# Pooling tiles between the modulations' pieces, another mix of split and whole pieces, four splits on another engine, and sums at other places in the heads

## The chip, the cores and the metric

One core of one Trainium2 chip. The metric is the device time of one execution in microseconds (us), and it is the lower the better. Engines are named as in the profile: PE (TensorE, matmuls; PEld are its weight loads), DVE (VectorE), ACT (ScalarE), POOL (GpSimd), SP (the engine whose queue issues most transfers).

## The reference, cut to what matters

The model is one step of a two-layer backbone over 640 tokens of width 1024: 512 latent tokens (a grid of 8 by 64) and 128 context tokens. Layer 0 mixes tokens by pooling, layer 1 by retention with 4 heads; an MLP with a squared ReLU (4096 wide) follows each. Every sub-layer is normed, then scaled and shifted, and its result is gated:

```
mod = silu(cond) @ w_ada[i] + b_ada[i]          # cond: c (latent) or c_ctx (context)
sh_a, sc_a, g_a, sh_m, sc_m, g_m = split(mod, 6)
h = rmsnorm(x, norm_mix_w[i]) * (1 + sc_a) + sh_a
mix = pool_mixer(h) if i == 0 else retention_mixer(h)
x = x + g_a * mix
h = rmsnorm(x, norm_mlp_w[i]) * (1 + sc_m) + sh_m
x = x + g_m * square(relu(h @ mlp_w1[i])) @ mlp_w2[i]
```

So each layer needs six modulations, each a product of two vectors (two kinds of token) with a 1024 x 1024 matrix of `w_ada`: 4 MB of weights per modulation, 48 MB in all, for almost no arithmetic. The pooling mixer takes, per group of 256 channels, the mean over a window of 2, 4, 8 or 16, less the token itself, through a 256 x 256 matrix.

## The kernel before, in words

Activations lie transposed, as eight tiles d = 0..7 of 128 channels by 640 tokens, in two halves of 320 tokens. Products with float32 precision are made of three matmuls of a reduced float32 type (`mm3`, L205 to L207): each operand is split into a high part (`S.copy` on ACT, L144) and the low remainder (a subtraction on DVE, or on POOL where a call says so, L145).

**Modulations.** `ada` (L272) computes them in steps, as a generator. A modulation has two halves of 512 columns and each half four pieces of 256 rows; a step handles one piece. The five modulations of layer 0 that are needed first come in the order 1, 0, 2, 4, 3: 40 pieces, with one load of 1 MB for each two pieces on SP's queue, into five buffers. A letter of `MODES` (L50) says how a piece is multiplied: `p` whole, in plain float32, without other engines; `v` split by ACT and DVE into two parts that PE multiplies with a split vector. All are the matmuls of L283. A piece is multiplied one step late (`LAG`). When a half's four pieces are done, ACT copies the row (L287) and PE turns it (L293, `turn`), one step later again.

**The opening's order** is written out in `PLAN` (L52): `a2` is two steps of the modulations, `l` and `v` load tables, `w3` is pooling tile 3 (`pooled`, L608), and `PLAN[1]` to `PLAN[8]` stand between the eight products of the pooling mixer (`pool_add`, L675). The function `run` (L646) reads a word with `map(int, word[1:])`, which goes through the digits of the word one by one:

```
def run(plan):
    for word in plan.split():
        {"w": pooled, "a": astep, "v": vectors, "l": load_tables}[word[0]](*map(int, word[1:]))
```

So `a10` calls `astep(1, 0)`, and the second argument of a `step` (L402) is `until`: it goes on until modulation 0 is in a set of pairs, which never is, and thus through all pieces to the end of the generator. Pooling tile 0 stands behind all 40 pieces, and the later words `a2` and `a1` find nothing to do.

A pooling tile takes five transposes on PE (L621, L622), eight matmuls with a window matrix (L630) and one for the context (L632), two activations on ACT (L637), four operations on DVE (L638, L639) and a split (L144, L145). Each two tiles share `group` (L593): a load of `iv` on ACT's queue (L596), the window matrix `pm` on DVE (L601), and the split of four 128 x 256 inputs into tiles of the tag `t` (L603 to L605), of which there are seven. The tile also needs modulations 1 and 0 (`a0` and `mod[0][0]`). Matmuls, transposes and sums write PSUM banks of one tag, of which there are eight. A framework orders each engine's instructions by its own estimates; buffers of one tag are given out in program order.

**Then** come the products `pool_add` with `add_to_x` (L500), the sums of squares (`Squares`, L421), the reciprocal root (`rsqrt`, L147 to L159, on DVE), and `norm_tile` (L475), whose tiles (`h0h`, `h0l`, ...) feed the MLP (`mlp`, L749).

**Weights of the MLP** are split by `weights` (L186); `OTHER[i]` (L59) says how many of the first blocks of 128 columns of layer i's MLP have their subtraction on POOL: none in layer 0, four in layer 1.

**The heads.** In layer 1 four modulations are made by `ada_sums` (L375): a step loads 1 MB, multiplies and adds it up on DVE (16 operations of 128 x 256, L387 and L389) in two accumulators that exist once, and the next step first turns the result on PE (four transposes, L394) and reduces it on DVE (L395). There are 16 such sums, so 17 steps. They stand in the loop over heads (L1149 on): a step behind the preparation of attention, one behind the product `gate(0)`, one behind `gate(1)`, one behind `gated`, and in head 0 one more before the output projection, which needs modulation 2 of layer 1. Between heads, `values` (L981) and `queries_keys` make the next head's inputs.

Of the kernel before, what the change touches and what calls it, by code (L numbers as in the profile page):

```python
# [9 lines left out]
F32 = mybir.dt.float32  # L10
# [36 lines left out]

MODES = ("pppp ppvv", "vvpv vpvv", "vvpv vpvp", "vpvp ppvp", "vppv vpvp")  # L50
MODE5 = "s s"
PLAN = ("a2 l a4 v a10 w0 a2 w1 a2 w2 a2 w3 a2 w4 a2 w5 a2 w6 a2 w7",  # L52
        "a1", "a1", "a1", "a1", "a1", "a1", "a1", "a1")
LAG = 1
FIRST = "x x x x x"
LATE = (False, True)
TURN = 5
BACK = 5
OTHER = (0, 4)  # L59
AHEAD = 1  # L60
FREE = 5

# [48 lines left out]
def hybrid_kernel(ctx: ExitStack, tc: tile.TileContext, x_prompt, x_sample, state_ret, c, c_ctx, w_ada, b_ada,  # L111
# [6 lines left out]
    def nm(s):  # L118
        uid[0] += 1
        return f"{s}_{uid[0]}"  # L120
# [254 lines left out]
    def ada_sums(works, place):  # L375


        for i, m in works:
            for q in range(4):
                col = m * D + q * 256  # L380
                w = load(w_ada[i, :, col:col + 256], (8, 256))
                acc = place()
                for k in range(KD):
                    for j in range(2):
                        by = c4[:, k, j:j + 1]
                        if k == 0:
                            V.tensor_scalar(acc[j], w[:, k], by, None, ALU.mult)  # L387
                        else:
                            V.scalar_tensor_tensor(acc[j], w[:, k], by, acc[j], ALU.mult, ALU.add)  # L389
                yield  # L390
                pt = bank()
                for j in range(2):
                    for k in range(2):
                        T.transpose(pt[:, (2 * j + k) * 128:(2 * j + k + 1) * 128], acc[j][:, k * 128:(k + 1) * 128], ident)  # L394
                V.tensor_reduce(mod[i][m][:, q * 2:q * 2 + 2, :], pt.rearrange("p (j n k) -> p n j k", j=2, n=2),  # L395
                                axis=AX.X, op=ALU.add)
            ob = O_B + i * 48 + m * KD
            V.tensor_tensor(mod[i][m], mod[i][m], vec[:, ob:ob + KD].unsqueeze(2).to_broadcast([128, KD, 2]), ALU.add)
            ready.add((i, m))

    def stepper(gen):
        def step(n=1, until=None):  # L402
            while n if until is None else until not in ready:
                try:
                    next(gen)
                except StopIteration:
                    return
                n -= 1
        return step
# [62 lines left out]
    def h_tiles(d, dt=F32R):  # L472
        return [hp.tile([128, TOK], dt, tag=f"h{d}{e}", name=nm(f"h{d}{e}")) for e in "hl"]
# [56 lines left out]
    def follow(sq, norm, items):  # L530


        r = []

        def products(item, h, mid=None):
            return gemm([w() for w in item[0]], item[1], h, mid)

        out = products(items[0], 0, lambda: r.append(sq.rstd()))
        splits = []
        for d in range(KD):  # L540
            splits.append(norm(1, d, r[0]))
            if d:
                splits[d - 1]()
        splits[-1]()
        items[0][2](0, out)
        for h in range(2):
            for item in items[1 - h:]:
                item[2](h, products(item, h))


    with tc.tile_pool(name="pool", bufs=1) as pp:
# [56 lines left out]
        def pooled(d):  # L608

            if not a0:  # L610
                astep(until=(0, 0))
                a0.append(scale_of(0, 1, O_MIX))
            g = d // 2
            if d % 2 == 0:
                grp[g] = group(g)
            iv, pm, xh, xl = grp[g]
            cols = slice(d * 128, (d + 1) * 128)
            sub = slice(d % 2 * 128, d % 2 * 128 + 128)
            ps, pq, pr = bank(), bank(), bank()
            for i in range(4):  # L620
                T.transpose(ps[:, i * 128:(i + 1) * 128], xt[i][:, cols], ident)  # L621
            T.transpose(pq[:, 0:128], xt[4][:, cols], ident)  # L622
            for i in range(4):

                w = WINDOWS[g]
                lo, hi = max(0, 2 * i - w // 2 + 1), min(ROWS, 2 * i + w // 2 + 2)
                lo, hi = (0, ROWS) if i == 0 else (min(lo, ROWS - 4), max(hi, min(lo, ROWS - 4) + 4))
                o = SPAN // 2 - 1 - 2 * i
                for e, z in enumerate((xh, xl)):
                    T.matmul(pr[:, lo * GRID_W:hi * GRID_W], z[i // 2][:, i % 2, sub], pm[:, o + lo:o + hi, :],  # L630
                             start=(i == 0 and e == 0), stop=(i == 3 and e == 1))
            T.matmul(pq[:, 128:256], xt[4][:, cols], win_sb[:, g * SEQ:(g + 1) * SEQ], start=True, stop=True)  # L632
            n_ = h_tiles(d, F32)[0]
            t = pp.tile([128, TOK], F32, tag="df", name=nm("df"), bufs=2)
            for j, cols, z, mean in ((0, slice(0, LAT), ps, pr), (1, slice(LAT, TOK), pq[:, 0:128], pq[:, 128:256])):
                sc_, sh_ = a0[0][:, d, j:j + 1], mod[0][0][:, d, j:j + 1]
                S.activation(n_[:, cols], z, AF.Identity, scale=sc_, bias=sh_)  # L637
                V.scalar_tensor_tensor(t[:, cols], mean, sc_, iv[:, cols], ALU.mult, ALU.mult)  # L638
                V.scalar_tensor_tensor(t[:, cols], t[:, cols], sh_, n_[:, cols], ALU.add, ALU.subtract)  # L639
            diff.append(split(t, *h_tiles(d)))  # L640
# [4 lines left out]

        def run(plan):  # L646
            for word in plan.split():
                {"w": pooled, "a": astep, "v": vectors, "l": load_tables}[word[0]](*map(int, word[1:]))

        run(PLAN[0])  # L650
        astep(until=(0, 2))
# [258 lines left out]
    with tc.tile_pool(name="ret", bufs=1) as rp:  # L910
# [70 lines left out]
        def values(hd):  # L981

            out = [bank() for _ in range(5)]
            c0 = 2048 + hd * DV
            for e in range(2):
                st = load(ret_w_in[0, e * 512:(e + 1) * 512, c0:c0 + 512], (4, 512))
                for f in range(2):
                    w = split_w(st[:, 2 * f:2 * f + 2])
                    for i in range(5):
                        for k in range(2):  # L990
                            hh = [z[:, i * 128:i * 128 + 128] for z in h1t[e * 4 + f * 2 + k]]
                            first, last = e == 0 and f == 0 and k == 0, e == 1 and f == 1 and k == 1
                            T.matmul(out[i], hh[0], w[0][:, k, :], start=first, stop=False)  # L993
                            T.matmul(out[i], hh[1], w[0][:, k, :], start=False, stop=False)  # L994
                            T.matmul(out[i], hh[0], w[1][:, k, :], start=False, stop=last)  # L995
            vs = [centre(out[i], *[rp.tile([128, DV], F32R, tag=f"v{i}{e}", name=nm("v")) for e in "hl"])
                  for i in range(4)]
            vpr = t5()
            vpc = rp.tile([128, DV], F32, tag="vpc", name=nm("vpc"))
            S.copy(vpr, out[4])  # L1000
            V.tensor_scalar(vpc, vpr, mean_of(vpr), None, ALU.add)
            return vs, split(vpr, t5().bitcast(F32R), t5().bitcast(F32R)), vpc
# [133 lines left out]

        qk, pairs, _ = queries_keys(0)
        follow(sq, norm1, pairs)
        vv = values(0)
        h2 = []  # L1140

        def norm2(h, d, r):
# [1 line left out]
                h2.extend([scale_of(1, 4, O_MLP + KD), mod[1][3], [h_tiles(d) for d in range(KD)]])  # L1144
            return norm_tile(h, d, r, *h2)

        step1 = stepper(ada_sums([(1, 2), (1, 4), (1, 3), (1, 5)], lambda: [rp.tile(
            [128, 256], F32, tag=f"acc{j}", name=nm("acc")) for j in range(2)]))
        for hd in range(HEADS):  # L1149
            gate = gates(hd)  # L1150
            final = states(hd, qk[1], vv[1])
            next(final)
            attn = attention(hd, *qk, vv[0], vv[2])
            step1()
            sg = [gate(0, between=final)]
            step1()
            sg.append(gate(1, between=final))
            step1()
            us = gated(hd, gate, sg, *attn())
            step1()  # L1160
            get = weights(ret_w_out[0, hd * DV:(hd + 1) * DV])
            if hd < HEADS - 1:
                vv = values(hd + 1)
                if hd == 0:
                    step1(until=(1, 2))
                for n in range(KD):
                    for h in range(2):
                        add_to_x(n, h, gemm([get(n)], us, h)[0], mod[1][2])
                qk, _, singles = queries_keys(hd + 1)
                for u in singles:  # L1170
                    u()
            else:
                sq = tail(lambda n, h: gemm([get(n)], us, h)[0], mod[1][2], normed(norm2))
# [74 lines left out]
```

## Time and profile before

| what | value |
|---|---|
| runs shown | 1634.32, 1642.6, 1639.77 us; median 1639.77 us |
| profiled execution, its own time | 1639.26 us |
| its span in the profile | 1637.4 us (mean granted clock of PE 0.991) |
| PE busy | 1585.1 us, 97% of the span |
| DVE busy | 1181.8 us, 72% |
| ACT busy | 703.3 us, 43% |
| POOL busy | 22.6 us, 1% |
| read from memory | 161.43 MB, 103 GB/s over the span |

The profile shows one execution. Busy times say how long an engine had an instruction; a wait is the idle time in front of an instruction, with what ended it. The granted clock is 1.00 at PE's full clock (2.4 GHz) and 0.50 at its half clock (1.2 GHz); a value between is a mean over a stretch.

### The profile page before, as it was taken

The page shows a single profiled execution, that of the slowest core. Times are in us where ns is not written, and L with a number is a line of the kernel's source. Part 1 is how long each engine was busy: PE and PEld are TensorE (multiplying, and loading weights), DVE is VectorE, ACT ScalarE, POOL GpSimd, SP SyncE. Part 2 cuts the span into 40 slices and gives each one's busy share as a digit, 9 for nine tenths or more (in the row PEclk, how much of TensorE's full clock was granted, in tenths as well). Part 3 has the DMA queues.
Part 4 walks back from the last instruction along what each step waited for, and adds up shares of the span by engine and source line. Part 5 has one row for each costly group of instructions (what it writes and reads, how often), then busy time and mean ns, then how long its engine had stood idle before and what let it go on. Part 6 is the DMA issues. An engine that isn't in the chain of part 4 may idle for free.

```text
span 1637.4 us, 24591 instructions
## 1 busy us (share of the span) xinstructions
PE 1585.1 (97%) x9897; PEld 1478.8 (90%) x9897; DVE 1181.8 (72%) x2295; ACT 703.3 (43%) x1287; POOL 22.6 (1%) x30
## 2 busy tenths in 40 slices
PE   7988999999999999999999999999999999999998
PEld 2278999999999998889889988998899999999998
DVE  4499997677667687886986688678966574564654
ACT  5665525416237364333442433243464262351540
POOL 0000000000000000000000000000200000000000
PEclk9999999999999999999999999999999999999999
DMA  9813431333333213324313142223122032131311
GB/s 352 296 57 129 155 104 52 109 124 103 109 98 104 78 43 126 115 78 129 129 52 129 63 145 102 78 91 116 52 77 78 27 109 98 52 104 52 109 59 65
DMA packets 137954, 169.83 MB, mean 104 GB/s; under 512 B 3512, under 2 KB 111472, under 8 KB 137840
## 3 DMA queue, kind: packets, MB, share of 16 engines
q1 hardware_dynamic: 134800, 161.28, 30.0%
q0 software_dynamic: 1312, 4.20, 0.8%
q10 hardware_dynamic: 1728, 2.78, 0.5%
q8 instruction: 78, 1.28, 0.3%
q14 instruction: 36, 0.29, 0.1%
HBM read 161.43 MB, written 6.82 MB: 103 GB/s over the span
## 4 chain that ended last, share of the span: by engine, by line
PE 83%; DVE 8%; DMA 5%; ACT 3%; issue 1%; ACTq 0%; DVEq 0%; SPq 0%
PE ps L205 24%; PE ps L206 24%; PE ps L207 24%; DMA wst<-in_mlp_w_dram 2%; PE ps L995 2%; PE ps L993 2%; PE ps L994 2%; PE ps L283 2%; DVE wlo L145 2%; ACT whi L144 1%; DMA wst<-in_w_ada_dram 1%; DVE acc L389 1%; PE ps L394 1%; DVE xall L500 1%; PE ps L630 1%
## 5 line engine op out<-in xcount | busy, mean ns | idle before, releaser
L144 ACT CAST whi<-wst 128x1024 fp32r<-128x1024 f32 x242 | 251.2, 1047 | 467.0 <-PE ps L206 263.2
L145 DVE TENSOR_TENSOR wlo<-wst,whi 128x1024 fp32r<-128x1024 f32 x238 | 288.1, 1221 | 118.7 <-ACT whi L144 118.0
L206 PE MATMUL ps<-a,whi 128*128 128x320 f32 x896 | 276.9, 310 | 0.8 <-DVE a L145 0.8
L205 PE MATMUL ps<-a,whi 128*128 128x320 f32 x896 | 277.1, 310 | 0.2 <-ACT a L144 0.2
L207 PE MATMUL ps<-a,wlo 128*128 128x320 f32 x896 | 276.2, 309 | 0.0
L500 DVE SCALAR_TENSOR_TENSOR xall<-ps,mod,xall 128x320 f32<-128x320 f32 (+2 forms) x288 | 116.0, 434 | 160.3 <-PE ps L207 159.5
L206 PEld LDWEIGHTS ps<-a,whi 128*128 128x128 f32 x896 | 168.0, 188 | 2.0 <-DVE a L145 1.8
L205 PEld LDWEIGHTS ps<-a,whi 128*128 128x128 f32 x896 | 168.0, 188 | 0.4 <-ACT a L144 0.4
L207 PEld LDWEIGHTS ps<-a,wlo 128*128 128x128 f32 x896 | 168.0, 188 | 0.0
L389 DVE SCALAR_TENSOR_TENSOR acc<-wst,c,acc 128x256 f32<-128x256 f32 x336 | 136.1, 477 | 0.0
L207 PE MATMUL ps<-tq,wlo 128*128 128x320 f32 x288 | 89.0, 309 | 0.0
L205 PE MATMUL ps<-tq,whi 128*128 128x320 f32 x288 | 89.0, 309 | 0.0
L206 PE MATMUL ps<-tq,whi 128*128 128x320 f32 x288 | 89.0, 309 | 0.0
L145 DVE TENSOR_TENSOR a<-t,a 128x320 fp32r<-128x320 f32 x128 | 61.8, 487 | 23.8 <-ACT a L144 23.0
L206 PE MATMUL ps<-A,whi 128*128 128x320 f32 x256 | 79.0, 309 | 0.0
L205 PE MATMUL ps<-A,whi 128*128 128x320 f32 x256 | 78.8, 311 | 0.0
L207 PE MATMUL ps<-A,wlo 128*128 128x320 f32 x256 | 78.5, 309 | 0.0
L855 ACT ACTIVATE t<-t 128x320 f32<-128x320 f32 x128 | 60.5, 473 | 1.3
L144 ACT CAST a<-t 128x320 fp32r<-128x320 f32 x128 | 58.5, 457 | 1.3
L435 ACT ACTIVATE t<-xall 128x320 f32<-128x320 f32 x56 | 26.1, 470 | 70.8 <-DVE xall L500 69.8
L207 PEld LDWEIGHTS ps<-tq,wlo 128*128 128x128 f32 x288 | 54.1, 188 | 0.0
L205 PEld LDWEIGHTS ps<-tq,whi 128*128 128x128 f32 x288 | 54.1, 188 | 0.0
(423 smaller groups left out, 4036.7 us busy)
## 6 DMA issues: line engine op xcount, KB each, us to landing
wst<-in_mlp_w_dram SPq DMA_DIRECT2D x64, 1024.0 KB, 5.3
wst<-in_w_ada_dram SPq DMA_DIRECT2D x46, 1024.0 KB, 5.3
wst<-in_ret_w_in_dram SPq DMA_DIRECT2D x24, 1024.0 KB, 5.2
wst<-in_ret_w_out_dram SPq DMA_DIRECT2D x8, 1024.0 KB, 5.1
t<-in_state_ret_dram SPq DMA_DIRECT2D x16, 256.0 KB, 4.0
out_dram<-t POOLq DMA_DIRECT2D x16, 256.0 KB, 2.6
xt<-in_x_sample_dram SPq DMA_DIRECT2D x4, 512.0 KB, 4.5
both<-in_w_ada_dram SPq DMA_DIRECT2D x2, 1024.0 KB, 7.3
```

What stands on the lines that cost most here:

```text
L144: S.copy(hi, src)
L145: sub.tensor_tensor(lo, src, hi.bitcast(F32), ALU.subtract)
L205: T.matmul(out, wh, ah, start=first, stop=False, skip_group_check=more)
L206: T.matmul(out, wh, al, start=False, stop=False, skip_group_check=more)
L207: T.matmul(out, wl, ah, start=False, stop=last, skip_group_check=more)
L283: T.matmul(pa, lhs[:, kk + k, :], z[:, k, :], start=first and k == 0 and j == 0, stop=last and k == 1 and j == len(w) - 1)
L389: V.scalar_tensor_tensor(acc[j], w[:, k], by, acc[j], ALU.mult, ALU.add)
L500: V.scalar_tensor_tensor(x, ps[:, cols], gate[:, d, j:j + 1], x, ALU.mult, ALU.add)
L855: S.activation(f, r, AF.Square)
L993: T.matmul(out[i], hh[0], w[0][:, k, :], start=first, stop=False)
L994: T.matmul(out[i], hh[1], w[0][:, k, :], start=False, stop=False)
L995: T.matmul(out[i], hh[0], w[1][:, k, :], start=False, stop=last)
```

## The change

Six edits. (1) `run` reads a word's digits as one number. (2) `a10` becomes `a5 a5`, and the plan's other words stay. (3) `MODES` gets other letters: 17 whole pieces where there were 20, one of them among the first 16 (8 before) and 16 among the last 24 (12 before). (4) `n_` in a pooling tile takes one buffer where `h_tiles` took a pair and used one. (5) `OTHER` becomes (0, 0): the four subtractions of layer 1's MLP go from POOL to DVE. (6) In the heads, a first step of the sums comes before `values(0)`; the step behind `gate(0)` stays in head 0 alone; and a step stands behind each `values(hd + 1)` where head 0 alone had one.

```diff
-MODES = ("pppp ppvv", "vvpv vpvv", "vvpv vpvp", "vpvp ppvp", "vppv vpvp")
+MODES = ("pvvv vvvv", "vvvv vvvv", "vpvp vpvp", "ppvp ppvp", "ppvp ppvp")
 MODE5 = "s s"
-PLAN = ("a2 l a4 v a10 w0 a2 w1 a2 w2 a2 w3 a2 w4 a2 w5 a2 w6 a2 w7",
+PLAN = ("a2 l a4 v a5 a5 w0 a2 w1 a2 w2 a2 w3 a2 w4 a2 w5 a2 w6 a2 w7",
         "a1", "a1", "a1", "a1", "a1", "a1", "a1", "a1")
...
-OTHER = (0, 4)
+OTHER = (0, 0)
...
-            n_ = h_tiles(d, F32)[0]
+            n_ = hp.tile([128, TOK], F32, tag=f"h{d}h", name=nm("n"))
...
-                {"w": pooled, "a": astep, "v": vectors, "l": load_tables}[word[0]](*map(int, word[1:]))
+                {"w": pooled, "a": astep, "v": vectors, "l": load_tables}[word[0]](*([int(word[1:])] if word[1:] else []))
...
         follow(sq, norm1, pairs)
+        step1 = stepper(ada_sums([(1, 2), (1, 4), (1, 3), (1, 5)], lambda: [rp.tile(
+            [128, 256], F32, tag=f"acc{j}", name=nm("acc")) for j in range(2)]))
+        step1()
         vv = values(0)
...
-        step1 = stepper(ada_sums([(1, 2), (1, 4), (1, 3), (1, 5)], lambda: [rp.tile(
-            [128, 256], F32, tag=f"acc{j}", name=nm("acc")) for j in range(2)]))
         for hd in range(HEADS):
...
             step1()
             sg = [gate(0, between=final)]
-            step1()
+            if hd == 0:
+                step1()
             sg.append(gate(1, between=final))
             step1()
             us = gated(hd, gate, sg, *attn())
...
                 vv = values(hd + 1)
-                if hd == 0:
-                    step1(until=(1, 2))
+                step1()
```

## Rows read from the trace of the kernel before

**Rows 1.** Windows: PE, PEld, DVE, ACT, POOL busy us; PEclk; DMA share; GB/s.

```profile
20.00:30.00 10.00, 8.78 (x27) 1.93 (x26) 2.87 (x4) 3.54 (x5) 0.00 (x0) 1.00 1.04 388
...
90.00:100.00 10.00, 4.60 (x22) 3.66 (x21) 10.00 (x23) 7.71 (x17) 0.00 (x0) 0.78 0.25 66
100.00:110.00 10.00, 10.00 (x53) 8.83 (x52) 9.35 (x19) 5.33 (x9) 0.00 (x0) 0.88 0.01 2
...
130.00:140.00 10.00, 5.20 (x19) 5.17 (x20) 10.00 (x21) 3.74 (x7) 0.00 (x0) 0.66 0.86 284
```

**Rows 2.** Timeline of PE, 43 to 84 us: start, length, line, operands, count.

```profile
44.28 0.41 PE L293 MATMUL ps<-tab_sb,t 4*128 4x4 f32 x4
...
64.59 1.88 PE L283 MATMUL ps<-wst,c 128*4 128x512 f32 x4
...
66.40 0.40 PE L283 MATMUL ps<-whi,chl 128*4 128x512 f32 x1
...
67.41 1.88 PE L283 MATMUL ps<-wst,c 128*4 128x512 f32 x4
```

**Rows 3.** Groups by line, 44.3 to 82.7 us: the pieces on PE.

```profile
L283 PE MATMUL ps<-wst,c 128*4 128x512 f32 x48 | 22.2, 592 | 0.0
...
L283 PE MATMUL ps<-wlo,chl 128*4 128x512 f32 x23 | 9.1, 394 | 0.9 <-DVE wlo L145 0.9
```

**Rows 4.** Timeline of PE, 82 to 136 us; the idle time before stands in brackets.

```profile
82.70 0.65 PE L621 MATMUL ps<-tab_sb,xt 128*128 128x128 f32 x4
...
97.66 0.77 PE L630 MATMUL ps<-pm,t 128*128 128x512 f32 x1 [5.36 <-ACT t L144]
...
109.25 0.39 PE L205 MATMUL ps<-h0h,whi 128*128 128x320 f32 x1
...
124.88 4.19 PE L455 MATMUL ps<-t,ones_d 128*128 128x320 f32 x14
134.80 1.17 PE L205 MATMUL ps<-h0h,whi 128*128 128x320 f32 x3 [5.73 <-ACT h0h L489]
```

**Rows 5.** Timeline of DVE, 82 to 136 us: the last tile's split; the first root's end.

```profile
114.43 0.82 DVE L145 TENSOR_TENSOR h7l<-df,h7h 128x640 fp32r<-128x640 f32 x1
...
132.07 0.48 DVE L159 SCALAR_TENSOR_TENSOR rstd<-t,rstd 128x320 f32<-128x320 f32 x1
```

**Rows 6.** Waits of PE, 690 to 1310 us: total us, times, longest.

```profile
PE ps L394 <- DVE acc L389: 6.9, 3, 2.3
```

**Rows 7.** Windows, head 3; columns as in the first group.

```profile
1080.00:1100.00 20.00, 17.47 (x104) 16.33 (x103) 17.91 (x44) 11.66 (x20) 2.15 (x4) 0.91 0.31 96
```

**Rows 8.** Timeline of PE, head 0: the transposes behind its first gate product.

```profile
645.91 0.60 PE L394 MATMUL ps<-tab_sb,acc 128*128 128x128 f32 x4
```

**Rows 9.** Timeline of DVE, head 0.

```profile
636.75 0.69 DVE L970 TENSOR_REDUCE cm<-t 128x1 f32<-128x512 f32 x1 [0.53 <-ACT t L1000]
...
647.91 5.62 DVE L389 SCALAR_TENSOR_TENSOR acc<-wst,c,acc 128x256 f32<-128x256 f32 x14
```

**Rows 10.** Timeline of POOL, 1100 to 1300 us: the last two of its four splits.

```profile
1179.86 6.10 POOL L145 TENSOR_TENSOR wlo<-wst,whi 128x1024 fp32r<-128x1024 f32 x2 [4.08 <-DVE xall L500]
```

**Rows 11.** Timeline of DVE, 1150 to 1206 us: one split, and four operations of root and norm.

```profile
1149.71 1.22 DVE L145 TENSOR_TENSOR wlo<-wst,whi 128x1024 fp32r<-128x1024 f32 x1
...
1169.92 2.70 DVE L156 SCALAR_TENSOR_TENSOR rstd<-t,rstd 128x320 f32<-128x320 f32 x1
...
1174.04 2.08 DVE L159 SCALAR_TENSOR_TENSOR rstd<-t,rstd 128x320 f32<-128x320 f32 x1
...
1181.66 2.08 DVE L493 SCALAR_TENSOR_TENSOR h3l<-t,mod,h3h 128x320 fp32r<-128x320 f32 x1
1183.67 2.64 DVE L487 SCALAR_TENSOR_TENSOR t<-xall,a,rstd 128x320 f32<-128x320 f32 x1
```

**Rows 12.** Windows at the start of layer 1's MLP; columns as in the first group.

```profile
1184.00:1188.00 4.00, 1.21 (x6) 0.71 (x5) 4.00 (x6) 1.03 (x2) 1.96 (x1) 0.99 0.20 41
1188.00:1192.00 4.00, 3.00 (x11) 3.00 (x12) 4.00 (x12) 2.06 (x4) 0.00 (x0) 0.50 0.66 225
```

## The prediction

> **What bounds the kernel now.** I read the page first: PE is busy for 97% of the span, so only its gaps, its half-clock stretches and its own work can give time back. The windows and the list of PE's waits then show where the gaps lie: in the opening, once in each of three heads, and where layer 1's MLP begins.
>
> The opening has four stretches. Up to about 44 us transfers set the pace: at 20 to 30 us the DMA engines are full while DVE has 2.87 us of work in ten [rows 1]. At 44.28 us modulation 0 is complete (the fourth turn) and the first pooling tile could start; it starts at 82.70 [rows 2, 4]. In between PE has nothing but pieces. Then the eight tiles come at once, DVE is full, 10.00 and 9.35 us of ten, and PE waits 5.36 us for inputs whose splits stand behind that work [rows 1, 4]. The products follow, and when PE has emptied its queue (124.88 + 4.19 = 129.07) it waits 5.73 us for the first normed tile, since DVE finishes the root only at 132.07 + 0.48 [rows 4, 5]. Half clock follows both waits: a mean clock c over W us means 2(1 - c)W at half, so 4.4 and 2.4 us at 90 to 110, and 6.8 at 130 to 140 [rows 1].
>
> So DVE's pooling work should be done while DVE is idle, and the mended plan does that.
>
> **The opening, in PE's work.** A whole piece takes 66.40 - 64.59 = 1.81 us, a split one 67.41 - 66.40 = 1.01 [rows 2]. From 44.28 on PE has 12 whole pieces (48 instructions, four each), 11 split ones (23 low parts, two each) [rows 3] and six turns of about 0.34 (an estimate from 0.41 for four overlapping matmuls [rows 2]): 21.7 + 11.1 + 2.0 = 34.8 of the 38.4 us up to 82.70, so 3.6 of waits. With the new letters there are 15 whole and 8 split: 27.2 + 8.1 + 2.0 = 37.3. The early pieces that are now split save PE time where transfers set the pace, so I count that at nothing; were their splits late there (a cast, and a subtraction of 1.22 us [rows 11]), modulation 0 would be complete 1 to 2 us later.
>
> Tiles and products take 129.07 - 82.70 = 46.4, less the wait of 5.36, less what half clock cost: the 2.3 us from 97.66 to 100 and the 2.4 in the next window, 4.7 at half, so 2.4 lost. That leaves 38.6.
>
> Without any wait PE is through at 44.3 + 37.3 + 38.6 = 120.2. I add 3.0 of waits (nearest the 3.6 that the pieces had; low 0, high 9, the 3.6 and the 5.36 both) and put the wait for the first normed tile at 3.5 (low 1, high 5.73): DVE has less queued, but the root's nine operations and the late splits of MLP weights stay. The MLP then starts at 126.7, not 134.80: **-8.1**. Of the 2.6 us that half clock cost behind 134.80 (5.2 us of busy PE [rows 1]) I give back half, -1.3. **Opening: -9.4**, between 0 and -15.
>
> The Trainium skill has a rule that speaks against whole pieces late: "FP8 and Floating Point Precision", TensorE Precision Notes, says that true float32 takes four passes through the array, while reduced float32 is read in truncated form. If a reduced product is one pass, an estimate from that page makes a whole piece twice a split one, not 1.81 to 1.01, and three more of them late would add 3.0 where I have 2.4; the rows decide for 2.4.
>
> What else of the tiles moves. DVE needs (114.43 + 0.82 - 82.70) / 8 = 4.1 us per tile [rows 4, 5], and PE (109.25 - 82.70 - 5.36 - 2.4) / 8 = 2.3 [rows 4] and 2.8 to 3.6 for the two pieces beside it. So PE stays the longer by 1 to 2 us; where a tile's pieces are split (1.22 more on DVE), they are even. SP's queue: the pool weights are asked for between piece loads, and the MLP's first loads behind the last of these; both have tens of us. ACT's queue issues the four `iv` loads among casts; the last two wait for a buffer that tile 1 or 3 has long given back: nothing, and with that cover gone a few us. One buffer in place of a pair for `n_`: nothing, as the other one was never written.
>
> **The heads.** Three times PE waits for sums at the transposes behind `gate(0)`, 6.9 us together [rows 6]. That step is gone in heads 1 to 3, and behind `gate(1)` the sums have had another product's time. Head 3 also spent 2 x 0.09 x 20 = 3.6 us at half clock [rows 7], so 1.6 lost on what was busy. Removed: 8.5.
>
> But head 0 gets a step more. Before, its first sums ran ahead of `values(0)`, and the transposes behind `gate(0)` came at 645.91 without a wait [rows 8]. Now the step before `values(0)` takes that place, and what these transposes read can be summed only once the accumulators have been turned, near 636.75, where DVE begins the head's preparation; that and one other sum go on to about 653.5 (647.91 + 5.62) [rows 9]. High end of a wait: 7.6, all sums behind the preparation. Low end: 2.3, the other heads' [rows 6]. I take the middle, 4.9, since DVE's list is like theirs but still holds the end of `values(0)`; with 1.0 of half clock, 5.9. **Heads: -2.6**, between -6.2 and +1.
>
> The steps before the output projections of heads 1 and 2 put 6 us of DVE in front of `add_to_x`, and a load on SP in front of the projection's weights. Head 0 has this already, and PE's waits there show none of it: nothing, at most 1 each.
>
> **Layer 1's MLP.** POOL makes four splits, the last two in 6.10 us [rows 10]. Meanwhile four DVE operations take 2.70, 2.08, 2.08 and 2.64 [rows 11], where such a one takes 0.48 [rows 5] and a norm's some 0.54: 7.4 us lost in the root and norm on which PE waits. On DVE the splits cost 4 x 1.22 = 4.9 [rows 11]. The chain is 2.5 shorter; PE idles 2.8 + 1.0 us in eight, with the clock at 0.50 behind [rows 12], 1.5 us lost. I take 2.5 and 1.0 of clock: **-3.5**, between 0 (all four splits in front of the first normed tiles) and -5.3, the idle and the clock together. POOL's queue keeps its output transfers.
>
> **Sum.** The profiled execution took 1639.26 us (1.9 around its span), 0.5 below the runs' median, which I neglect. -9.4 - 2.6 - 3.5 = -15.5: **1623.8 us**.
>
> **Rivals.**
> 1. *Interleaving brings its own waits.* Buffers go out in program order: seven tiles `t` serve the four split inputs of a group and the pieces' rows. If PE waits 3 us once per group, as it did for 5.36 in one, the opening loses 12 less the 3.0 counted: -0.4 there, -6.5 in all, 1632.8. For: that wait exists. Against: two pieces now stand between tiles. 0.19.
> 2. *Slower: tiles stop pieces.* PE takes its queue in order, so a tile whose banks wait for DVE also holds the pieces behind it. Eight tiles, each waiting DVE's 4.1 us, cost 33 less 3.0: +14.5 in all, 1653.8. It decides from 3.3 us a tile on ((15.5 + 3.0 + 8) / 8). Against: PE's share with two pieces is the longer. 0.05.
> 3. *The change does not do what it says*: the framework's order puts the tiles behind all pieces again. Then the opening has 37.3 - 34.8 = +2.5, in all -3.6, 1635.7. Against: tile 0 came right behind the last turn that precedes it in the program. 0.05.
> 4. *More*: no waits in the opening, 1 us in front of the normed tile, 2.3 in head 0, full clock: -14 - 6 - 5 = -25, 1614.3. 0.15.
>
> My forecast has 0.56. **Range**: 1612 to 1634 leaves out rivals 2 and 3, the far third of rival 1 and some of rival 4, 2 in 10. **Chances**: 0.5%, 8 us, is about what a measurement of this kernel can tell from no change. Faster are forecast, rival 4 and a third of rival 1: 0.77; slower rival 2, 0.05; the rest, 0.18, is the same.
>
> **What would show it.** Right: the first L621 near 45 us, DVE below full from 44 to 120, no wait over 2 us at L630, the MLP's first L205 near 127; no wait at L394 in heads 1 to 3, one of 2 to 7 us in head 0; no L145 on POOL, and roots at 0.5 an operation near 1160. Wrong: several waits of 3 us between tiles, a first L205 behind 131, or a head 0 that loses over 8.

## The result, and the profile after

The changed kernel took 1623.9 us (median of four runs, 1620.39 to 1624.59) and the kernel before, in four runs, 1640.9: a ratio of 0.9899, 95% interval 0.9868 to 0.9931. The forecast was 1623.8 us, 1612 to 1634, and a chance of 0.77 for faster. So sign and size came as forecast. Not all terms of the sum did: the opening gave more, the heads took where they should have given, and the two errors nearly cancel.

The profiled execution took 1624.59 us, its span 1622.7 (before 1639.26 and 1637.4). On the page, PE's busy time has hardly moved (1585.1 before), and POOL's has halved (22.6). What went is idle time, 52.3 us of the span before and 37.0 after; the mean granted clock is 0.992 where it was 0.991:

```profile
PE 1585.7 (98%) x9897; PEld 1477.2 (91%) x9897; DVE 1183.0 (73%) x2302; ACT 705.5 (43%) x1290; POOL 11.6 (1%) x26
```

**The opening**, the windows that answer to [rows 1]; columns as there:

```profile
20.00:30.00 10.00, 7.68 (x27) 2.49 (x27) 8.69 (x10) 7.39 (x9) 0.00 (x0) 0.67 1.05 387
...
70.00:80.00 10.00, 10.00 (x47) 5.64 (x46) 7.26 (x16) 9.36 (x21) 0.00 (x0) 1.00 0.64 210
...
90.00:100.00 10.00, 10.00 (x44) 4.99 (x44) 6.92 (x13) 3.83 (x8) 0.00 (x0) 1.00 0.48 166
100.00:110.00 10.00, 10.00 (x54) 6.93 (x53) 5.79 (x14) 2.79 (x6) 0.00 (x0) 1.00 0.37 111
...
130.00:140.00 10.00, 9.10 (x61) 8.70 (x60) 10.00 (x22) 2.98 (x8) 0.00 (x0) 1.00 0.12 28
```

From 50 to 120 us PE is full at full clock, and DVE, where it had 10.00 and 9.35 of ten, has 6.92 and 5.79 (5.79 to 9.54 in the seven windows). DVE's idle time that the tiles now fill lay before the first tile; a window of the kernel before, from modulation 0's turn to that tile, has DVE busy for 16.58 of 38.42 us:

```profile
44.28:82.70 38.42, 35.67 (x122) 8.42 (x121) 16.58 (x25) 22.50 (x36) 0.00 (x0) 1.00 0.83 290
```

After the change, PE's timeline, answering to [rows 2, 4], has:

```profile
43.22 0.41 PE L293 MATMUL ps<-tab_sb,t 4*128 4x4 f32 x4 [0.44 <-ACT t L287]
43.56 0.66 PE L621 MATMUL ps<-tab_sb,xt 128*128 128x128 f32 x4
...
119.49 1.88 PE L455 MATMUL ps<-t,ones_d 128*128 128x320 f32 x6
123.01 0.85 PE L205 MATMUL ps<-h0h,whi 128*128 128x320 f32 x4 [1.64 <-ACT h0h L489]
```

The first tile stands right behind modulation 0's turn (82.70 before), the wait of 5.36 at L630 is gone, that for the first normed tile is 1.64 instead of 5.73, and the MLP begins at 123.01 instead of 134.80.

**Head 0** is where the surprise lies. PE's timeline, inside `values(0)` and behind it:

```profile
598.71 0.33 PE L1008 MATMUL ps<-tab_sb,pr 128*128 128x128 f32 x1 [1.35 <-ACT pr L941]
599.46 0.66 PE L394 MATMUL ps<-tab_sb,acc 128*128 128x128 f32 x4 [0.42 <-DVE t L949]
600.85 0.47 PE L1008 MATMUL ps<-tab_sb,pr 128*128 128x128 f32 x1 [0.73 <-ACT pr L941]
...
601.97 0.63 PE L994 MATMUL ps<-whi,h1l 128*128 128x512 f32 x1
602.40 0.63 PE L995 MATMUL ps<-wlo,h1h 128*128 128x512 f32 x1
...
609.73 0.39 PE L993 MATMUL ps<-whi,h2h 128*128 128x512 f32 x1
609.95 0.39 PE L994 MATMUL ps<-whi,h2l 128*128 128x512 f32 x1
...
646.76 0.41 PE L394 MATMUL ps<-tab_sb,acc 128*128 128x128 f32 x2 [0.55 <-ACT sg L1034]
```

The windows at the first of these waits, columns as in [rows 1]:

```profile
600.00:605.00 5.00, 4.27 (x13) 3.29 (x12) 5.00 (x11) 1.47 (x5) 0.00 (x0) 0.50 0.06 12
605.00:610.00 5.00, 5.00 (x20) 4.05 (x19) 2.66 (x6) 0.00 (x0) 0.00 (x0) 0.81 1.03 338
```

Before, the two key transposes L1008 of head 0 came behind `values(0)`:

```profile
635.88 0.38 PE L1008 MATMUL ps<-tab_sb,pr 128*128 128x128 f32 x2
```

Now they and the first turn L394 stand among its first products, and wait there for ACT's and DVE's work on rope, the rotation of queries and keys by position (L941, L949): 2.50 us of waits. Behind them PE issues a product each 0.43 us (601.97 to 602.40) instead of each 0.22 (609.73 to 609.95): half clock.

**Layer 1's MLP.** Before, PE's three waits at its start were these, 5.4 us together:

```profile
1183.80 0.41 PE L206 MATMUL ps<-h3l,whi 128*128 128x320 f32 x1 [1.62 <-DVE h3l L493]
...
1186.96 0.42 PE L205 MATMUL ps<-h4h,whi 128*128 128x320 f32 x1 [2.17 <-ACT h4h L489]
...
1189.00 0.64 PE L206 MATMUL ps<-h4l,whi 128*128 128x320 f32 x1 [1.62 <-DVE h4l L493]
```

After the change no wait there is over 0.5 us, no L145 is on POOL, and DVE's root operation that took 2.70 [rows 11] takes 0.48:

```profile
1158.68 0.48 DVE L156 SCALAR_TENSOR_TENSOR rstd<-t,rstd 128x320 f32<-128x320 f32 x1
```

**Stage by stage.** The table cuts PE's time at five of its instructions: modulation 0's turn (L293 near 43 us), the MLP's L205 that waits for `h0h`, the first L993 of `values(0)` and of `values(1)`, and the first L465 near 1130. The column "first PE" is the start of PE's first instruction, and "rest of PE" ends with its last. Each row is one profiled execution. The last column is the median of the timed runs; letters alone, heads alone, splits on POOL and early letters old have one run each.

| kernel | first PE | to the turn | turn to MLP | to values(0) | head 0 | heads 1 to 3 | rest of PE | us |
|---|---|---|---|---|---|---|---|---|
| before | 6.22 | 38.06 | 90.52 | 472.61 | 91.68 | 437.82 | 494.96 | 1640.9 |
| after | 7.34 | 35.88 | 79.79 | 471.89 | 98.81 | 431.95 | 491.85 | 1623.9 |
| plan alone | 6.30 | 36.89 | 85.36 | 471.82 | 91.99 | 436.55 | 493.46 | 1629.74 |
| letters alone | 6.11 | 35.45 | 91.61 | 472.79 | 92.57 | 438.11 | 492.57 | 1636.44 |
| heads alone | 6.25 | 37.31 | 90.04 | 472.83 | 96.36 | 431.95 | 492.78 | 1636.26 |
| after, old heads | 6.22 | 35.15 | 79.79 | 471.05 | 92.66 | 438.23 | 489.62 | 1622.44 |
| after, step behind values(0) | 6.36 | 36.11 | 79.79 | 471.48 | 98.13 | 432.60 | 491.92 | 1623.55 |
| after, splits on POOL | 6.31 | 37.29 | 79.79 | 471.24 | 94.88 | 431.82 | 494.87 | 1623.72 |
| after, early letters old | 6.06 | 37.22 | 79.79 | 471.71 | 96.65 | 432.27 | 491.61 | 1622.31 |
| after again | 6.12 | 35.81 | 79.79 | 471.42 | 96.73 | 433.02 | 491.82 | 1621.47 |
| late step | 6.47 | 36.12 | 79.79 | 471.35 | 92.15 | 432.30 | 491.69 | 1617.88 |
| late step again | 6.09 | 35.77 | 79.79 | 471.73 | 91.88 | 433.32 | 491.59 | 1618.1 |
| late step, late splits | 6.12 | 36.28 | 78.26 | 470.74 | 92.65 | 432.94 | 492.39 | 1617.63 |

By it the change is +1.1 (the first input came later in that run), -2.2 and -10.7 (the opening), -0.7, +7.1 (head 0), -5.9 (heads 1 to 3), -3.1 (layer 1's MLP): -14.4 of the -14.7 in the span; the rest lies behind PE's end.

### The profile page after: what moved, and what is told of

Read it like the earlier page. It is cut to its first block, busy times and chain, and to the rows that moved or that the text cites. A ratio compares the mean times of both kernels' runs of the same rounds, so it can differ in the third digit from the quotient of the medians.

```text
span 1622.7 us, 24563 instructions
## 1 busy us (share of the span) xinstructions
PE 1585.7 (98%) x9897; PEld 1477.2 (91%) x9897; DVE 1183.0 (73%) x2302; ACT 705.5 (43%) x1290; POOL 11.6 (1%) x26
## 4 chain that ended last, share of the span: by engine, by line
PE 81%; DVE 7%; DMA 5%; ACT 5%; issue 1%; DVEq 0%; ACTq 0%; SPq 0%
PE ps L205 23%; PE ps L206 23%; PE ps L207 23%; DMA wst<-in_mlp_w_dram 3%; PE ps L283 3%; PE ps L995 2%; PE ps L994 2%; PE ps L993 2%; DVE wlo L145 2%; ACT whi L144 2%; DVE acc L389 1%; PE ps L630 1%; DMA xt<-in_x_sample_dram 1%; PE ps L465 1%; PE ps L394 1%
## 5 line engine op out<-in xcount | busy, mean ns | idle before, releaser
L145 DVE TENSOR_TENSOR wlo<-wst,whi 128x1024 fp32r<-128x1024 f32 x245 | 296.8, 1223 | 110.5 <-ACT whi L144 109.8
L206 PE MATMUL ps<-a,whi 128*128 128x320 f32 x896 | 276.9, 310 | 0.7 <-DVE a L145 0.7
L205 PE MATMUL ps<-a,whi 128*128 128x320 f32 x896 | 277.0, 310 | 0.4 <-ACT a L144 0.4
L206 PEld LDWEIGHTS ps<-a,whi 128*128 128x128 f32 x896 | 168.0, 188 | 2.1 <-DVE a L145 1.9
L205 PEld LDWEIGHTS ps<-a,whi 128*128 128x128 f32 x896 | 168.0, 188 | 0.7 <-ACT a L144 0.7
L205 PE MATMUL ps<-tq,whi 128*128 128x320 f32 x288 | 89.0, 309 | 0.0
L206 PE MATMUL ps<-tq,whi 128*128 128x320 f32 x288 | 89.0, 309 | 0.0
L145 DVE TENSOR_TENSOR a<-t,a 128x320 fp32r<-128x320 f32 x128 | 62.1, 489 | 23.3 <-ACT a L144 22.8
L206 PE MATMUL ps<-A,whi 128*128 128x320 f32 x256 | 78.9, 309 | 0.0
L205 PE MATMUL ps<-A,whi 128*128 128x320 f32 x256 | 78.9, 312 | 0.0
L205 PEld LDWEIGHTS ps<-tq,whi 128*128 128x128 f32 x288 | 54.1, 188 | 0.0
```

What stands on the lines that cost most here:

```text
L145: sub.tensor_tensor(lo, src, hi.bitcast(F32), ALU.subtract)
L205: T.matmul(out, wh, ah, start=first, stop=False, skip_group_check=more)
L206: T.matmul(out, wh, al, start=False, stop=False, skip_group_check=more)
```

## The experiments

The theory after the comparison, called A: the plan makes the opening's gain; the step ahead of `values(0)` makes head 0's loss; the other moves pay in heads 1 to 3; the splits off POOL pay in layer 1's MLP.

**Plan alone**, an edit of the kernel before.

```diff
-PLAN = ("a2 l a4 v a10 w0 a2 w1 a2 w2 a2 w3 a2 w4 a2 w5 a2 w6 a2 w7",
+PLAN = ("a2 l a4 v a5 a5 w0 a2 w1 a2 w2 a2 w3 a2 w4 a2 w5 a2 w6 a2 w7",
...
-                {"w": pooled, "a": astep, "v": vectors, "l": load_tables}[word[0]](*map(int, word[1:]))
+                {"w": pooled, "a": astep, "v": vectors, "l": load_tables}[word[0]](*([int(word[1:])] if word[1:] else []))
```

> The kernel before with the plan alone mended (two groups of five pieces, tiles between them); letters, heads and the last pair as before. Theory A (the plan makes the opening's gain, because the tiles fall into DVE's idle stretch): the MLP's first L205 comes near 123 to 125 us, as against 134.80 before and 123.01 after, the heads go as before, the time is 11 to 13 us below the kernel before, near 1628. Theory B (the new letters make the gain, by having whole pieces and no split to wait for late): the first L205 stays above 130 and the time is within 4 us of the kernel before.

Measured: 1629.74 us beside 1638.18 (ratio 0.9949, 0.9932 to 0.9966), the MLP's first L205 at 128.55. From the turn to the MLP that is 5.2 of the 10.7 us, less than A expected and more than B. PE's timeline shows what is left:

```profile
91.57 0.39 PE L283 MATMUL ps<-whi,chl 128*4 128x512 f32 x1 [4.70 <-ACT whi L144]
...
128.55 0.86 PE L205 MATMUL ps<-h0h,whi 128*128 128x320 f32 x4 [2.27 <-ACT h0h L489]
```

ACT's timeline in front of the first of these shows why:

```profile
84.39 1.91 ACT L659 ACTIVATE xall<-xall,gb 128x512 f32<-128x512 f32 x4
86.20 0.71 ACT L144 CAST h7h<-df 128x640 fp32r<-128x640 f32 x1
86.82 2.82 ACT L659 ACTIVATE xall<-xall,gb 128x512 f32<-128x512 f32 x6
89.54 1.98 ACT L144 CAST whi<-wst 128x1024 fp32r<-128x1024 f32 x2
```

A late split piece waits for its cast, which stands in ACT's queue behind the last tile's work and the bias terms of L659; the granted clock from 90 to 100 us is then 0.66. It is a wait of the kind that the prediction's rival 1 feared, but at one place instead of four, and for a cast instead of a buffer.

**Letters alone**, an edit of the kernel before.

```diff
-MODES = ("pppp ppvv", "vvpv vpvv", "vvpv vpvp", "vpvp ppvp", "vppv vpvp")
+MODES = ("pvvv vvvv", "vvvv vvvv", "vpvp vpvp", "ppvp ppvp", "ppvp ppvp")
```

> The kernel before with the new letters alone; all tiles still come behind all pieces. Theory A: the opening does not get shorter, the first L205 of the MLP lies between 134 and 138 us (three more whole pieces late, 2.4 us of PE, less what the late splits of DVE gave back). Theory B: the first L205 comes at 123 to 128 us. Under both, the layer-1 MLP keeps its four splits on POOL only if its letters there are untouched by this list; the heads go as before.

Measured: from the turn to the MLP 91.61, 1.1 more than before, with the waits of 5.35 and 5.73 us still there. (The first L205, at 133.17, is below what was expected since the turn came at 41.56.) So theory B falls. But neither edit does it alone: plan -5.2, letters +1.1, both together -10.7. Once the tiles stand between the pieces the letters are worth 5.6 us, since a whole piece asks nothing of ACT: from the plan alone to the changed kernel PE's waits in this stretch fall from 6.97 to 1.64, half clock that cost 3.4 is gone, and the three more whole pieces cost PE 3.2. Edit (4), the one buffer for `n_`, was in no run alone; with the plan alone, which still has the pair, PE's only waits in the stretch are the two shown, and neither is for `n_`.

**Old heads**: the sums of the heads at their old places. This and the next edits, but for the heads alone, are of the changed kernel.

```diff
+        vv = values(0)
         step1 = stepper(ada_sums([(1, 2), (1, 4), (1, 3), (1, 5)], lambda: [rp.tile(
...
-        step1()
-        vv = values(0)
...
-            if hd == 0:
-                step1()
+            step1()
...
-                step1()
+                if hd == 0:
+                    step1(until=(1, 2))
```

> The changed kernel with the sums of the heads at their old places. Theory A (the step put ahead of values(0) makes head 0 lose 7 us, and the other moves give 6 back in heads 1 to 3): head 0 keeps its lead of some 12.5 us over the kernel before up to its out-projection, heads 1 to 3 keep the three waits at L394, and the time is 1 to 2 us below the changed kernel, near 1622.5. Theory B (head 0 loses because what stands ahead of it now runs earlier, whatever the step does): head 0 loses its 7 us here too, nothing is gained in heads 1 to 3, and the time is 5 to 7 us above the changed kernel, near 1630.

Measured: 1622.44 us, 1.5 below the changed kernel (but 1.0 above its repeat below, so the time alone decides nothing); head 0 takes 92.66, heads 1 to 3 438.23. The stages are as theory A had them; B falls. Its rest of PE is 2.2 us shorter than in the changed kernel, with the same waits in the MLP. Some 1.5 of that is half clock in front of PE's end: the changed kernel has a clock of 0.66 at 1613 to 1618 us (PE busy for 4.51 of the five), this run 1.00 at 1609 to 1613, behind the same wait of 1.95 us.

**Late step.** The step goes from its place ahead of `values(0)` to one behind head 0's out-projection:

```diff
+        vv = values(0)
         step1 = stepper(ada_sums([(1, 2), (1, 4), (1, 3), (1, 5)], lambda: [rp.tile(
...
-        step1()
-        vv = values(0)
...
                         add_to_x(n, h, gemm([get(n)], us, h)[0], mod[1][2])
+                if hd == 0:
+                    step1()
                 qk, _, singles = queries_keys(hd + 1)
```

> The changed kernel without the step ahead of values(0); in its place head 0 has one more step behind its out-projection, ahead of the next queries and keys, so that the number of steps is the same. Theory A (as for the run before): head 0 keeps its lead, heads 1 to 3 gain their 6 us, the time is 5 to 8 us below the changed kernel, near 1617. Theory B (head 0 loses whatever the step does): within 1.5 us of the changed kernel. A third way: the steps that now come later in head 0 bring the wait at the transposes behind gate(0) back there, 2 to 7 us, and the gain is 0 to 5.

Measured: 1617.88 us, 6.0 below (the repeat below has both side by side), ratio to the kernel before 0.9875 (0.9857 to 0.9894). Head 0 keeps its lead (92.15) and heads 1 to 3 keep their gain (432.30). No turn in head 0 waits for sums.

**Step behind values(0).**

```diff
+        vv = values(0)
         step1 = stepper(ada_sums([(1, 2), (1, 4), (1, 3), (1, 5)], lambda: [rp.tile(
...
         step1()
-        vv = values(0)
```

> The changed kernel with the one step moved from ahead of values(0) to right behind it; nothing else. In the program's order the two key transposes (L1008) and the first turn (L394) of head 0 then stand behind all 40 products of values(0) instead of behind the first five of them. Theory A (the loss in head 0 comes from those transposes standing inside values(0), where rope has not made their inputs, and from the half clock behind their waits): values(0) takes as long as in the kernel before, head 0 keeps at least 5 of the 7 us, the time is 3 to 6 us below the changed kernel. The prediction's mechanism (the sums come too late for the turn behind gate(0), wherever that extra step stands ahead of the loop): a wait of 2 to 7 us at L394 in head 0, and the time is within 2 us of the changed kernel.

Measured: 1623.55 us, as the changed kernel, so A's forecast was wrong. With the 40 products of `values(0)` ahead of the transposes again, the three waits inside it go (one of 0.96 at L995 comes back that the kernel before has too, with 0.94), and the wait of the prediction appears, behind `gate(0)`, for DVE's sums; PE's timeline:

```profile
636.84 1.08 PE L394 MATMUL ps<-tab_sb,acc 128*128 128x128 f32 x4 [3.96 <-DVE acc L389]
```

and the windows around it:

```profile
630.00:635.00 5.00, 2.88 (x17) 2.27 (x15) 5.00 (x13) 4.96 (x9) 0.54 (x1) 1.00 0.38 120
635.00:640.00 5.00, 3.16 (x14) 3.14 (x15) 5.00 (x13) 0.55 (x2) 1.07 (x2) 0.66 0.69 224
```

Head 0 takes 98.13. So the extra step costs head 0 at both places ahead of the loop; only how differs.

**Heads alone**: on the kernel before, with its plan, letters and POOL splits, the heads' edits of the change.

```diff
+        step1 = stepper(ada_sums([(1, 2), (1, 4), (1, 3), (1, 5)], lambda: [rp.tile(
+            [128, 256], F32, tag=f"acc{j}", name=nm("acc")) for j in range(2)]))
+        step1()
         vv = values(0)
...
-            step1()
+            if hd == 0:
+                step1()
...
-                if hd == 0:
-                    step1(until=(1, 2))
+                step1()
```

> The kernel before with the new places of the heads' sums alone. Theory A: head 0, from the first product of values(0) to the first of values(1), takes 7 us more than before, the three waits at L394 in heads 1 to 3 are gone and give 5 to 6 back by the first product of layer 1's attention, so that the time is within 2 us of the kernel before. Prediction's sum for this part: -2.6, from -6.2 to +1.

Measured: head 0 +4.7, heads 1 to 3 -5.9, 1636.26 us beside 1638.93. The same three waits stand inside `values(0)` (1.34, 0.42, 0.73), so they do not come from the work ahead of head 0. The 7 us that were expected are 4.7. In this run half clock behind the waits cost 1.7 us where it cost 3.1 in the changed kernel's first profile.

**Splits back on POOL.**

```diff
-OTHER = (0, 0)
+OTHER = (0, 4)
```

> The changed kernel with the four splits of layer 1's MLP back on POOL. If they alone account for that stage: four splits (L145) on POOL, DVE's root and norm operations near 1160 us back at 2.1 to 2.7 us from 0.5, three waits of 1.6 to 2.2 us at L205 and L206, and 3 to 3.5 us more between the root's first product (L465) and the end of the span, near 1627.5. If it was DVE's cast work from other parts of the change: the operations stay at 0.5 us and the stage is within 1 us of the changed kernel.

Measured: the rest of PE 494.87, 3.0 more. POOL's timeline has the splits again, of which the first two:

```profile
1154.27 2.41 POOL L145 TENSOR_TENSOR wlo<-wst,whi 128x1024 fp32r<-128x1024 f32 x1 [69.80 <-ACT whi L144]
1157.78 2.41 POOL L145 TENSOR_TENSOR wlo<-wst,whi 128x1024 fp32r<-128x1024 f32 x1 [1.10 <-DVE t L157]
```

On DVE's timeline the operations that start beside them are long, those before and between short:

```profile
1153.67 0.48 DVE L155 SCALAR_TENSOR_TENSOR t<-t 128x320 f32<-128x320 f32 x1
1154.33 2.70 DVE L156 SCALAR_TENSOR_TENSOR rstd<-t,rstd 128x320 f32<-128x320 f32 x1
1157.29 0.47 DVE L157 TENSOR_TENSOR t<-rstd 128x320 f32<-128x320 f32 x1
...
1158.45 2.09 DVE L159 SCALAR_TENSOR_TENSOR rstd<-t,rstd 128x320 f32<-128x320 f32 x1
```

PE waits 1.50 at L205 and 2.77 at L206 there, and 0.45 and 0.50 between: 5.2 us in four waits, where three of 1.6 to 2.2 were expected. The one time, 1623.72, is 3.8 below the 1627.5 that were expected, mostly because in this run head 0 lost only 3.2: its waits are the same (1.33, 0.42, 0.72), and the granted clock behind them is 1.00. Beside the 1623.9 of the changed kernel, that time alone would have said that the splits cost nothing.

**Early letters old.**

```diff
-MODES = ("pvvv vvvv", "vvvv vvvv", "vpvp vpvp", "ppvp ppvp", "ppvp ppvp")
+MODES = ("pppp ppvv", "vvpv vpvv", "vpvp vpvp", "ppvp ppvp", "ppvp ppvp")
```

> The changed kernel with the letters of the first two modulations as before (seven whole pieces of sixteen there instead of one), the three later ones new. Theory C (splitting the early pieces leaves PE behind the transfers by less, so that modulation 0 is complete sooner): its turn comes 1.5 to 2.5 us later, counted from PE's first instruction (38 us instead of 36), the stretch from the turn to the MLP stays at 79.8, and the MLP starts 1.5 to 2.5 later. The prediction's count (nothing, as transfers set the pace there): the turn stays at 36 us from PE's first instruction.

(The old letters have eight whole pieces among those sixteen, not seven.) Measured: 37.22 us from PE's first instruction to the turn; from there 79.79 to the MLP, as in the changed kernel. Over all runs, kernels with the old early letters have 36.89 to 38.06 (four, mean 37.4), those with the new ones 35.15 to 37.29 (nine, mean 36.0, and all but one below 36.3). So the early splits give some 1.4 us rather than nothing, less than theory C wanted; as runs with the same early letters differ by 2.1 us in this stretch, the size is not settled. Early splits were late in the changed kernel, as the prediction feared:

```profile
20.87 0.59 PE L283 MATMUL ps<-whi,chl 128*4 128x512 f32 x1 [4.33 <-ACT whi L144]
```

Another wait of 1.45 follows at 22.91, and the granted clock at 20 to 30 us is 0.67, where it was 1.00 [rows 1]. Modulation 0 was complete no later for it; what makes up for it was not tried.

**After again, and late step again**, on one chip.

> The changed kernel once more, to see what of head 0's loss belongs to the kernel and what to the run. The three waits inside values(0) should come as before, 1.35, 0.42 and 0.73 us, and the stretch from modulation 0's turn to the MLP should take 79.8 us. Theory A2 (the waits are the kernel's, the half clock behind them differs from run to run): head 0 takes between 94.9 us, no half clock, and 98.8 us, all of it, as against 91.7 in the kernel before. If head 0's loss were fixed by the order of the instructions: 98.8 again. Time 1620 to 1625.

> The changed kernel with the extra step behind head 0's out-projection instead of ahead of values(0), once more and beside the changed kernel on the same chip. Theory A: no waits inside values(0), no half clock there, head 0 takes 92 to 92.5 us, the time is 4 to 7 us below that of the changed kernel in the same rounds. If the first comparison was chance: within 2 us of it.

Measured: the changed kernel 1621.47 us (1621.03 to 1623.4; ratio 0.9892, 0.9878 to 0.9907), the late step 1618.1 (1616.25 to 1619.97; ratio 0.987, 0.9855 to 0.9884). The difference is 3.4 us, under the 4 that A wanted, and no run of the one lies among those of the other. With the late step head 0 took 91.88, without the waits. In the changed kernel it took 96.73 with the same waits (1.33, 0.42, 0.73), so 98.8 is not fixed by the order. The window in which the first profile had a clock of 0.50 here has 0.66, and the next one is at 1.00:

```profile
600.00:605.00 5.00, 5.00 (x17) 3.97 (x16) 4.91 (x8) 0.35 (x1) 0.00 (x0) 0.66 0.41 122
605.00:610.00 5.00, 5.00 (x24) 4.14 (x23) 2.97 (x9) 0.00 (x0) 0.00 (x0) 1.00 0.91 298
```

**Late step, late splits**: the late step with two more splits in the last modulation.

```diff
-MODES = ("pvvv vvvv", "vvvv vvvv", "vpvp vpvp", "ppvp ppvp", "ppvp ppvp")
+MODES = ("pvvv vvvv", "vvvv vvvv", "vpvp vpvp", "ppvp ppvp", "pvvp pvvp")
```

> The kernel with the late step, and two of the five whole pieces of the last modulation split (the letters pvvp pvvp for ppvp ppvp). From modulation 0's turn to the end of the products PE has no gap, so its own work sets this stretch. Theory A (there DVE has 3 to 4 us of ten free, so two more splits are hidden): PE saves 2 x 0.8 us and the stretch from the turn to the MLP falls from 79.8 to about 78.2, the time by 1.6 us. Rival (a late split waits for a cast or a subtraction that stands behind other work of ACT or DVE, as for 4.7 us with the old letters): a wait of 1 to 5 us at L283 and a stretch of 80 to 85 us.

Measured: the stretch from the turn falls to 78.26, no late split waits, and the rival falls. But the wait for the first normed tile grows, as PE's timeline shows:

```profile
120.66 0.85 PE L205 MATMUL ps<-h0h,whi 128*128 128x320 f32 x4 [2.27 <-ACT h0h L489]
```

PE's work in the stretch thus fell by 79.79 - 1.64 - (78.26 - 2.27) = 2.16 us for two pieces, and 0.63 of it went into that wait. The normed tile needs the root, which DVE finishes at L159, and DVE's order has changed: the other half's L150, which waits for PE's sums of squares, now stands in front of L159, where it stood behind; why was not tried. DVE's timeline of this run:

```profile
118.42 0.49 DVE L150 TENSOR_SCALAR rstd<-ps 128x320 int32<-128x320 int32 x1 [1.15 <-PE ps L455]
118.83 0.48 DVE L159 SCALAR_TENSOR_TENSOR rstd<-t,rstd 128x320 f32<-128x320 f32 x1
```

The plan alone has the same order and the same wait of 2.27. The time, 1617.63 us (1617.1 to 1618.39; ratio 0.9868, 0.9852 to 0.9885), can't be told from that of the late step.

## Why the prediction was right, and which of its steps were not

**Opening: -9.4 forecast, -11.8 at the MLP's start and -12.5 at `values(0)`.** The mechanism was right: tiles in DVE's idle stretch, no wait at L630, the first L621 right behind the turn. DVE was below full, as forecast, at 5.79 to 9.54 of ten. The sizes were off in three terms of the stretch behind the turn, forecast as 126.7 - 44.3 = 82.4 and measured as 79.79. Waits among pieces and tiles: 3.0 forecast, none came. The wait for the normed tile: 3.5, and it was 1.64. PE's work: 37.3 + 38.6 = 75.9, and it was 79.79 - 1.64 = 78.15. Of the 2.2 that are missing there, 0.9 were missing before the change: PE is busy for 35.67 us from 44.28 to 82.70, where the prediction's count of pieces and turns came to 34.8, so the waits there were 2.75 and not 3.6. Another part lies in the price of a piece. It was read as 1.81 whole and 1.01 split, but a piece between other products has edges:

```profile
94.03 0.31 PE L207 MATMUL ps<-h3h,wlo 128*128 128x320 f32 x1
94.18 0.40 PE L283 MATMUL ps<-whi,chl 128*4 128x512 f32 x1
...
95.11 0.31 PE L205 MATMUL ps<-h2h,whi 128*128 128x320 f32 x1
...
95.70 0.31 PE L206 MATMUL ps<-h3l,whi 128*128 128x320 f32 x1
95.84 0.31 PE L207 MATMUL ps<-h3h,wlo 128*128 128x320 f32 x1
96.08 1.88 PE L283 MATMUL ps<-wst,c 128*4 128x512 f32 x4
97.89 0.41 PE L205 MATMUL ps<-h4h,whi 128*128 128x320 f32 x1
98.14 0.31 PE L206 MATMUL ps<-h4l,whi 128*128 128x320 f32 x1
```

These are lines of PE's timeline after the change. A split piece costs 95.11 - 94.18 = 0.93 and leaves the products' pitch of 0.15 alone. A whole one costs 1.81, and the pitch on either side of it is 0.24 and 0.25: 0.19 more, 2.00 together. The difference is 1.07; the late splits gave 1.08 each, and the three whole pieces of the new letters took 3.2, where 2.4 was charged. Those two parts make 1.7 of the 2.2; the rest was not traced. By the rule of the Trainium skill that the prediction weighed ("FP8 and Floating Point Precision", TensorE Precision Notes: four passes for true float32) a whole piece was estimated at twice a split one. The rows now say 2.00 to 0.93, so that estimate was nearer than the 1.81 to 1.01 that was taken.

The early splits were counted at nothing (some 1.4 us gained, not settled). From the MLP's start to `values(0)`, -1.3 was forecast for half clock and -0.7 came: the clock at 130 to 140 is 1.00, so all of the 2.6 came back, but 1.9 was lost again, 0.91 of it in a new wait for `h0h` at L205, at 138.46; the rest was not traced.

The letters' part in it was not seen. The prediction charged three more late whole pieces as a cost of 2.4; with the plan the new letters save 5.6, because a late split piece of the old ones waits in ACT's queue for its cast. Rival 1 named such a wait and put it on buffers.

**Heads: -2.6 forecast, +1.3 came.** In heads 1 to 3 the three waits at L394 went, and the clock at 1080 to 1100 is 1.00: 8.5 forecast, 5.9 came. The waits at L394 gave their 6.9 back and the clock the 1.6 that was counted, but three new waits of 0.3 to 0.8 us at L205, for `r`, take 1.5, and PE's busy time without the cost of half clock is 1.1 longer (430.2 less 1.6 before, 429.7 after); where that comes from was not traced. In head 0 a loss of 5.9 was forecast and one of 7.1 came, but the step that named its place failed: "what these transposes read can be summed only once the accumulators have been turned, near 636.75". The framework pulled turn and key transposes forward into `values(0)`, and they waited there for rope. The sign that the prediction gave, a wait of 2 to 7 us at L394 in head 0, did not come (0.42 and 0.55). Head 0's waits are 4.2 us (2.50 in `values(0)`, 0.55 for ACT's `sg`, 0.86 at L205 for `r`, two small ones), where they were 1.1 (0.94 of them at L995, gone now): 3.1 more. Half clock takes 0.50 x 4.27 + 0.19 x 5.00 = 3.1, and PE has 1.0 more of work, with 16 transposes L394 for 12. That is the 7.1. So the size came near the 5.9 by another way than the one forecast. With the step one line lower the mechanism of the prediction appears as it was told, with 3.96 us for a forecast of 4.9. What makes the framework choose one or the other was not tried.

**Layer 1's MLP: -3.5 forecast, -3.1 came**, and 3.0 of it left when the splits went back to POOL. The mechanism was right. The waits gave 3.4 (5.4 before, 2.0 after), where 2.5 was counted, and the clock nothing, where 1.0 was counted: the small waits that remain (five of 0.2 to 0.5 us near 1172) come with half clock all the same, 0.68 and 0.50 in the two windows of 4 us from 1172 on.

**Rivals.** 2 (tiles stop pieces) did not come: PE has no wait from 45 to 121 us. 3 (the order stays) neither: L621 at 43.56. 4 (more) was nearer for the opening (no waits, 1.64 for its 1 at the normed tile, -12.5 for its -14), and wrong for head 0, where it had a wait of 2.3 and a gain. A sum of -15.5 for -14.7 in the profile is thus right by a forecast of -9.4 that was 3 too small and one of -2.6 that was 4 too good. The way of the opening and of the MLP was foreseen; that the total came out within a microsecond was luck.

## What to carry to other kernels

Work for a side engine belongs where that engine is idle, and then the pieces beside it should not need the same engines: the order alone was worth 5 us from the turn to the MLP, the mix of pieces alone nothing, both together 11. A step that is moved ahead of a loop can pull others with it in a framework that orders the queues itself, so look in the changed trace for where its followers have gone, not only for the step. Where a wait brings half clock, judge an edit by its stage in the trace: whole times of this kernel hid a difference of 3 us.

## What the runs showed of the hardware

The same three waits, 2.5 us together, were followed by half clock of very different length: none in one run (head 0 in 94.88 us), a clock of 0.66 over 5 us in three (96.36, 96.65 and 96.73), 0.50 and 0.81 over two such windows in the first profile (98.81). From modulation 0's turn to the MLP the eight executions with this plan and the same late letters took 79.79 us each, while the stretch up to that turn took 35.15 to 37.29 us in the nine kernels with the new early letters. And DVE operations of 0.48 us took 2.70 and 2.09 when they started beside a split of 2.41 on POOL, and one between the two splits took 0.47.
